# A Strassen block product for the last layer's gate and up projections

## The chip, the cores and the metric

The kernel runs on one core of one Trainium2 chip. The metric is the device time of one execution in microseconds (us). Before the change the median of three runs is 1853.85 us (1850.95 to 1854.17).

## The reference, cut to what matters

Two layers of a backbone over 512 latent tokens (and 256 context tokens, which the second layer's feed-forward does not need). Each layer is a mixer and a SwiGLU feed-forward; the change lies in the feed-forward of the second layer (called layer 1) and in what joins it to the mixer:

```
x = x + mod[2] * (o_lat @ w_out)                    # the mixer's output projection, 1024 -> 1024
h = modulate(rmsnorm(x, norm_ffn_w), mod[3], mod[4])
gate, up = split(h @ ffn_w_in)                      # 1024 -> 2 x 2816
x = x + mod[5] * ((silu(gate) * up) @ ffn_w_out)    # 2816 -> 1024
```

Everything is 32-bit. For TensorE the kernel splits each operand into a rounded high part and the remainder (tiles with h and l at the end of their names, type fp32r), and takes each product as three matmuls: high by high, high by low, low by high.

## The kernel before, in words

Tokens lie on the free axis, channels on the 128 partitions: 1024 channels are KD = 8 blocks `d`, the 2816 hidden channels are NH = 22 blocks. All matmuls are issued by the helper `mm` (L194), so they share that line; tensor_tensor operations of VectorE are recorded on L201, its scalar_tensor_tensor on L214, ScalarE's activations on L222, DMAs on L225 and the cast of a loaded weight to its high part on L251. Tiles are told apart by name: `wr` is a weight as it came from memory, `wh` and `wl` its split, `hx` the normalized input of a projection, `hf` a hidden block, `hhi` and `hlo` its split, `x` the residual stream, `mm` and `wk` PSUM tiles (four buffers each). A scheduler turns the program order into one instruction order per engine; each engine then works its own list strictly in order and waits on semaphores.

**The end of the mixer, `out_norm` (L625 to L692).** The output projection works on two token halves of NC = 256 columns: 8 blocks d, 8 k and 3 products of 256 columns each, for half 0 and then for half 1. Beside it run the weights' loads, the norm of half 0 (`stats`, `spread`), and `hx`, which for each block d makes the normalized, modulated input and its split. The norm of half 1 is left to a generator `rest`, which the feed-forward calls step by step.

**The feed-forward of layer 1, `ffn` (L1173 to L1244).** For each of 22 hidden blocks it loads the gate's and the up projection's weight (512 KB each), casts and splits them (ScalarE, VectorE), and makes 2 x 8 x 3 matmuls of 512 columns. Silu of the gate times up gives a hidden block, which is split again. Blocks are taken in groups of 8, 7 and 7 (`FFN_GROUPS`); `group_out` then multiplies a finished group with the output weights (8 blocks d, 3 matmuls of 512 for each hidden block of the group) and adds the result to the residual. It is put behind the second block of the next group. The first hidden block of all is done in two halves of 256 columns, since the norm of the second half comes later.

**Layer 0 does the same product in another way: `block_ffn` (L1313 to L1395).** There the tokens are two halves of HT = 384 columns, the 1024 input channels two halves of 4 blocks, and gate and up are the two halves of the output: a 2 x 2 block product. In place of 8 half-size products it makes 7 of them, by a Strassen scheme (product numbers 1, 2, 6, 7, 5, 4, 3 in the order of the program), each 4 k x 3 matmuls of 384 columns. Its price is sums: of the weights (`block_sums`: s1, s2, s3 and one in place, four additions of 128 x 512 per hidden block, and the splits of all of them), of the inputs (`block_operands`, once: 36 VectorE operations on half blocks after the normalized input stands) and of the results (copies `ha`, `hb` and additions out of PSUM). The feed-forward's input in layer 0 has to stand whole before the products that need sums of it can run.

Of the kernel before, what the change touches and what calls it, by code (L numbers as in the profile page):

```python
# [9 lines left out]
F32 = mybir.dt.float32  # L10
# [9 lines left out]
P = 128  # L20
D = 1024
KD = D // P
NL = 512
# [11 lines left out]
FFN_GROUPS = (8, 7, 7)  # L35
# [3 lines left out]
BLOCK_ROWS = 3  # L39
V_EARLY = (1,)  # L40
# [112 lines left out]
class Kern:  # L153
# [471 lines left out]
    def out_norm(self, pw, o, xt, sa, sb):  # L625
# [3 lines left out]
        act = ([], [])  # L629
        for d in range(KD):  # L630
            if d % 4 == 0:
                h = [K.t(K.bp, (P, 4, NT), "hx", F32R, bufs=4) for _ in range(2)]
            for a, x in zip(act, h):
                a.append(x[:, d % 4, :NL])
# [40 lines left out]
        for d in range(1, 4):  # L675
            out(1, d)
        r = spread(r)
# [4 lines left out]

        def rest():
            r = stats(1)
            yield
            r = spread(r)
            yield
            for d in range(KD):
                hx(1, r, d)
            yield  # L690

        return act, rest()  # L692
# [480 lines left out]
    def ffn(self, l, act, xt, regions, done=None, rest=None):  # L1173
        K = self
        lat = regions == 1
        n = NL if lat else NT
        pend = []
        hp = K.hp
        start = 0

        def group_out(g0, hs):
            for d in range(KD):
                nh = len(hs)
                w = K.wload(K.I["ffo"][l, d][:, g0:g0 + nh, :], (nh, P))
                pl = K.mmps()
                segs = [(pl, 0, NL, True)]
                if not lat:
                    pc = K.wkps()
                    segs = K.halves(pl, pc)
                K.proj_fm(w, ([x[0] for x in hs], [x[1] for x in hs]), segs)  # L1190
                g = K.modc[l][:, 40 + d, :]
                if lat:
                    K.stt(xt[:, d, :NL], pl, g[:, 0:1], xt[:, d, :NL])
                else:
                    for p, c, r in K.parts(pl, pc):
                        K.stt(xt[:, d, c], p, g[:, r:r + 1], xt[:, d, c])
                if done and g0 + nh == NH:
                    done(d)

        for gn in FFN_GROUPS:  # L1200
            hs = []
            for j in range(gn):
                if j == 2 and pend:
                    group_out(*pend.pop())
                ps, pcs = [], []
                late = []
                if rest:
                    next(rest)
                for gu in range(2):
                    w = K.wload(K.I["ffi"][l, start + j, gu], (KD, P))  # L1210
                    p = K.mmps()
                    segs = [(p, 0, NL, True)]
                    if rest:
                        segs = [(p[:, :NC], 0, NC, True)]
                        late.append((w, [(p[:, NC:], NC, NL, False)]))
                    if not lat:
                        pcs.append(K.wkps())
                        segs = K.halves(p, pcs[gu])
                    K.proj_fm(w, act, segs)
                    ps.append(p)  # L1220
                    if rest:
                        next(rest)
                if rest:
                    rest = None
                    for w, segs in late:
                        K.proj_fm(w, act, segs)
                f = K.t(hp, (P, n), "hf", bufs=2)
                if lat:
                    K.act(f, ps[0], AF.Silu)
                    K.mul(f, f, ps[1])  # L1230
                else:
                    for a in range(2):
                        c = slice(HT * a, HT * a + HT)
                        K.act(f[:, c], (ps, pcs)[a][0][:, :HT], AF.Silu)
                        K.mul(f[:, c], f[:, c], (ps, pcs)[a][1][:, :HT])
                hi = K.t(hp, (P, n), "hhi", F32R, bufs=10)
                lo = K.t(hp, (P, n), "hlo", F32R, bufs=10)
                K.A.copy(out=hi, in_=f)
                K.sub(lo, f, hi)
                hs.append((hi, lo))  # L1240
                K.bg(3, "mod")
            pend.append((start, hs))
            start += gn
        group_out(*pend.pop())  # L1244
# [702 lines left out]
```

## Time and profile before

| what | value |
|---|---|
| median of three runs | 1853.85 us (1850.95 to 1854.17) |
| the profiled execution | 1851.05 us, of which 1849.3 us lie between its first and last instruction |
| TensorE busy | 1765.9 us, 95% of the span |
| VectorE busy | 1192.7 us, 64% |
| ScalarE busy | 689.4 us, 37% |
| mean granted clock of TensorE | 0.973 of full speed |

The busy share is an average over the whole program. The change touches the last fifth of it: the output projection's last columns fall at 1480 us, and from there to the end VectorE works about a third of the time and TensorE is the only engine without gaps. A matmul's busy time is counted until its results are out, so two neighbours overlap in the records; what a matmul costs in a stream is the distance between starts.

### The profile page before, as it was taken

To read this page: it belongs to the slowest core of one execution; us is meant where nothing else is said; L and a number is where in the kernel's file an instruction comes from. 1 tells how busy PE (TensorE), PEld (TensorE's weight loads), DVE (VectorE), ACT (ScalarE), POOL (GpSimd) and SP (SyncE) were. 2 spreads that over 40 slices of the span, in tenths; PEclk is the share of its full clock that TensorE was granted. 3 is DMA by queue.
4 is the path that set the end of the run, shared out by engine and by line. 5 is a ranking of instruction groups with operands and counts; after the bars stand their busy time and mean duration, and the time that the engine had idled before them with its cause. 6 is when DMAs were issued, how large, how long until landed. Compare 5 with 4: busy or idle time off the path is not lost.

```text
span 1849.3 us, 28533 instructions
## 1 busy us (share of the span) xinstructions
PE 1765.9 (95%) x11047; PEld 1595.6 (86%) x11047; DVE 1192.7 (64%) x2422; ACT 689.4 (37%) x1417; POOL 87.1 (5%) x94
## 2 busy tenths in 40 slices
PE   4999999999899799999999998999999999999999
PEld 4988899988697799999999996788998988888887
DVE  5686696548847999988856467579555753333333
ACT  2453534235614642424242324322443432223231
POOL 0011001100002000000000000100003100000000
PEclk9999999779999899999999998999999999999999
DMA  8343466445374448496826265532532523333332
GB/s 334 113 153 125 125 212 187 99 153 185 112 226 184 167 129 284 163 313 207 284 89 199 72 213 193 182 109 74 176 110 93 182 80 93 101 94 96 99 95 96
DMA packets 123076, 286.71 MB, mean 155 GB/s; under 512 B 28729, under 2 KB 45545, under 8 KB 119228
## 3 DMA queue, kind: packets, MB, share of 16 engines
q1 hardware_dynamic: 122940, 284.88, 47.1%
q8 instruction: 87, 1.43, 0.3%
q14 instruction: 49, 0.40, 0.1%
HBM read 228.96 MB, written 55.87 MB: 154 GB/s over the span
## 4 chain that ended last, share of the span: by engine, by line
PE 76%; DVE 13%; DMA 5%; ACT 3%; issue 3%; POOL 0%; SPq 0%; POOLq 0%; DVEq 0%; ACTq 0%
PE mm L194 51%; PE wk L194 23%; DMA wm<-in_modt_dram 2%; PE wk L198 1%; DVE wj L214 1%; PE sa L194 1%; DVE wl L201 1%; DVE ac L214 1%; ACT wh L251 1%; PE sa L198 1%; DVE ul L201 1%; DVE x L201 1%; DVE ivt L201 0%; DMA rvt<-rvD 0%; DVE ivy L201 0%
## 5 line engine op out<-in xcount | busy, mean ns | idle before, releaser
L194 PE MATMUL mm<-hx,wh 128*128 128x512 f32 (+2 forms) x1976 | 526.5, 361 | 8.5 <-ACT hx L409 4.3
L194 PEld LDWEIGHTS mm<-hx,wh 128*128 128x128 f32 x1976 | 358.7, 190 | 54.2 <-ACT hx L409 4.5
L194 PE MATMUL mm<-hx,wl 128*128 128x512 f32 (+2 forms) x988 | 329.2, 360 | 0.5 <-DVE wl L201 0.5
L201 DVE TENSOR_TENSOR wl<-wr,wh 128x1024 fp32r<-128x1024 f32 (+1 forms) x159 | 193.3, 1215 | 186.4 <-ACT wh L251 178.6
L251 ACT CAST wh<-wr 128x1024 fp32r<-128x1024 f32 (+1 forms) x137 | 142.8, 1043 | 419.7 <-PE mm L194 411.6
L194 PE MATMUL mm<-wh,hx 128*128 128x256 f32 x1216 | 231.5, 289 | 2.6 <-DVE sv L964 1.1
L194 PEld LDWEIGHTS mm<-hx,wl 128*128 128x128 f32 x988 | 184.9, 190 | 23.6 <-issue 4.1
L194 PEld LDWEIGHTS mm<-wh,hx 128*128 128x128 f32 x1216 | 193.6, 194 | 5.5 <-issue 1.7
L194 PE MATMUL mm<-wl,hx 128*128 128x256 f32 x608 | 175.0, 289 | 0.0
L194 PEld LDWEIGHTS mm<-wl,hx 128*128 128x128 f32 x608 | 117.9, 194 | 1.0 <-issue 0.6
L1319 ACT CAST uh<-wr 128x512 fp32r<-128x512 f32 (+1 forms) x93 | 56.0, 605 | 155.6 <-PE wk L194 86.8
L214 DVE SCALAR_TENSOR_TENSOR wj<-wm,cb 128x1024 bf16<-128x1024 f32 x80 | 97.8, 1222 | 10.3 <-DMA wm<-in_modt_dram 9.8
L214 DVE SCALAR_TENSOR_TENSOR x<-mm,modc,x 128x256 f32<-128x256 f32 (+3 forms) x72 | 40.6, 585 | 86.2 <-PE mm L194 85.0
L194 PE MATMUL mm<-hx,uh 128*128 128x384 f32 x344 | 87.4, 334 | 0.6 <-ACT ha L1347 0.6
L201 DVE TENSOR_TENSOR ul<-wr,uh 128x512 fp32r<-128x512 f32 (+1 forms) x93 | 61.6, 665 | 18.5 <-ACT uh L1319 18.3
L194 PE MATMUL mm<-hhi,wh 128*128 128x512 f32 x176 | 68.5, 389 | 0.0
L194 PE MATMUL mm<-hlo,wh 128*128 128x512 f32 x176 | 68.5, 389 | 0.0
L194 PE MATMUL mm<-hhi,wl 128*128 128x512 f32 x176 | 68.5, 389 | 0.0
L1319 ACT CAST uh<-us 128x512 fp32r<-128x512 f32 x63 | 38.3, 623 | 76.8 <-PE wk L194 48.9
L194 PEld LDWEIGHTS mm<-hx,uh 128*128 128x128 f32 x344 | 62.0, 188 | 1.0 <-ACT ha L1347 1.0
L201 DVE TENSOR_TENSOR hf<-hf,mm 128x512 f32<-128x512 f32 x22 | 15.1, 688 | 71.6 <-PE mm L194 71.6
L194 PE MATMUL mm<-hlo,uh 128*128 128x384 f32 x176 | 58.9, 335 | 0.0
(447 smaller groups left out, 3426.8 us busy)
## 6 DMA issues: line engine op xcount, KB each, us to landing
wr<-in_ffi_dram SPq DMA_DIRECT2D x88, 512.0 KB
xr<-xr SPq DMA_DIRECT2D x80, 384.0 KB
wm<-in_modt_dram SPq DMA_DIRECT2D x56, 512.0 KB
wm<-in_modw_dram SPq DMA_DIRECT2D x20, 1024.0 KB
wr<-in_ffo_dram SPq DMA_DIRECT2D x32, 256.0 KB
wr<-in_rett_dram SPq DMA_DIRECT2D x16, 512.0 KB
wr<-in_ffo_dram SPq DMA_DIRECT2D x16, 448.0 KB
wr<-in_abf_dram SPq DMA_DIRECT2D x12, 512.0 KB
```

The source lines that it names most:

```text
L194: self.T.matmul(out=out, lhsT=l, rhs=r, start=start, stop=stop, skip_group_check=True)
L198: self.T.transpose(out, in_, self.ident[:n, :n])
L201: (eng or self.V).tensor_tensor(out=out, in0=a, in1=b, op=op)
L214: self.V.scalar_tensor_tensor(out=out, in0=a, scalar=s, in1=b, op0=op0, op1=op1, **kw)
L251: self.A.copy(out=hi, in_=raw)
L1319: A.copy(out=hi, in_=src)
```

## The change

`ffn` goes away. Layer 1's feed-forward is done by `block_ffn`, which now takes the half width as an argument (h = 384 in layer 0, NC = 256 in layer 1), the groups (6, 6, 5, 5 in layer 1), and the place of a finished group's output (behind the first block of the next group, `lead` = 1). `out_norm` builds the operands for the seven products instead of one input: half 0 gives the operands of products 1 and 2 while the second half of the output projection runs; the norm of half 1 is taken at once, and then `block_combos` makes the operands of 6, 7, 5, 4 and 3, in that order. The weights of a hidden block come from `block_pairs`, which casts and splits them in pieces of 1024, 512 and 1024 columns (tiles `f`, `e`, `f`); for hidden block 0 it is called inside the output projection.

```
-    def ffn(self, l, act, xt, regions, done=None, rest=None):
...
+    def out_norm(self, pw, hq, o, xt, sa, sb):
...
+        def split(n, k, x):
+            hi, lo = (o[:, k] for o in ops[n])
+            K.A.copy(out=hi, in_=x)
+            K.sub(lo, x, hi)
+
         def hx(t, r, d):
             c = slice(NC * t, NC * t + NC)
-            hd, ld = act[0][d][:, c], act[1][d][:, c]
-            x = K.t(K.sx, (P, NC), "hxt", bufs=4)
+            x = xp[d][:, c]
             K.stt(x, xt[:, d, c], sa[:, d, 0:1], r, ALU.mult, ALU.mult)
-            K.act(hd, x, AF.Identity, bias=sb[:, d, 0:1])
-            K.stt(ld, x, sb[:, d, 0:1], hd.bitcast(F32), ALU.add, ALU.subtract)
+            K.act(x, x, AF.Identity, bias=sb[:, d, 0:1])
+            if t == 0:
+                split(1 if d < 4 else 2, d % 4, x)
...
         for d in range(1, 4):
             out(1, d)
+        ready[0] = K.block_pairs(1, 0, hq)
         r = spread(r)
         for d in range(4, KD):
             out(1, d)
             for e in (2 * d - 8, 2 * d - 7):
                 hx(0, r, e)
...
+        r = spread(stats(1))
+        room((5, 4, 3))
+        for d in range(KD):
+            hx(1, r, d // 2 + 4 * (d % 2))
+        K.block_combos(xp, NC, split)
+        return ops, ready
...
+    def block_pairs(self, l, j, pool):
+        K = self
+        w, src, S, g = K.block_sums(l, j, pool, 2)
+
+        def split(x, n, tag):
+            hi, lo = (K.t(pool, (P, n, P), tag + c, F32R, bufs=2) for c in "hl")
+            K.A.copy(out=hi, in_=x)
+            K.sub(lo, x, hi)
+            return [(hi[:, i:i + 4], lo[:, i:i + 4]) for i in range(0, n, 4)]
+
+        w[6], w[7] = split(S[:, :8], 8, "f")
+        w[5], = split(src[5], 4, "e")
+        w[3], w[4] = split(src[0], 8, "f")
+        return w
...
-        for gn in BLOCK_GROUPS:
+        for gn in groups:
             hs = []
             for j in range(gn):
-                if j == 2 and pend:
+                if j == lead and pend:
                     group_out(*pend.pop())
...
-        act, rest = K.out_norm(K.pool(s, "wo", side="right"), od, xt, *K.scale_shift(1, "ffn", nr=1))
-        K.ffn(1, act, xt, 1, lambda d: K.dma(out[:, d], xt[:, d]), rest)
+        hq = K.pool(s, "hq1")
+        ops, ready = K.out_norm(K.pool(s, "wo", side="right"), hq, od, xt, *K.scale_shift(1, "ffn", nr=1))
+        K.block_ffn(1, NC, ready, ops, K.hp, hq, LAST_GROUPS, LAST_HID, 1, xt=xt, done=lambda d: K.dma(out[:, d], xt[:, d]))
```

The order of the instructions changes with it on VectorE and ScalarE; everything before `out_norm` keeps its order.

VectorE, in the second half of the output projection. Before, beside the additions to the residual (`x`) there stand the reciprocal root of half 0's norm (`nrst`, `nrsy`) and the split of the first gate weight (`wl`):

```order
L235 TENSOR_SCALAR nrst_14713<-nms_14711 128x2
L236 TENSOR_SCALAR nrsy_14714<-nrst_14713 128x2
L201 TENSOR_TENSOR nrst_14713<-nrsy_14714 128x2
L214 SCALAR_TENSOR_TENSOR nrst_14713<-nrst_14713,nms_14711 128x2
L214 SCALAR_TENSOR_TENSOR nrsy_14714<-nrst_14713,nrsy_14714 128x2
L214 SCALAR_TENSOR_TENSOR x_14514<-mm_14726,modc_10_88,x_14514 128x256
L201 TENSOR_TENSOR nrst_14713<-nrsy_14714 128x2
L214 SCALAR_TENSOR_TENSOR nrst_14713<-nrst_14713,nms_14711 128x2
L214 SCALAR_TENSOR_TENSOR nrsy_14714<-nrst_14713,nrsy_14714 128x2
L201 TENSOR_TENSOR wl_14902<-wr_14899,wh_14901 128x1024
```

Now, from the fifth addition of the first half on, the weight sums of hidden block 0 (`us` and, in place, the up weight `wr_14789`) and the splits of the sums (`el`, `fl`):

```order
L202 TENSOR_TENSOR us_14796<-wr_14789 128x512
L215 SCALAR_TENSOR_TENSOR x_14514<-mm_14635,modc_10_88,x_14514 128x256
L202 TENSOR_TENSOR us_14796<-us_14796,wr_14788 128x512
L202 TENSOR_TENSOR us_14796<-wr_14788,wr_14789 128x512
L215 SCALAR_TENSOR_TENSOR x_14514<-mm_14652,modc_10_88,x_14514 128x256
L202 TENSOR_TENSOR wr_14789<-wr_14788,us_14796 128x512
L202 TENSOR_TENSOR el_14806<-us_14796,eh_14805 128x512
L215 SCALAR_TENSOR_TENSOR x_14514<-mm_14669,modc_10_88,x_14514 128x256
L202 TENSOR_TENSOR fl_14802<-us_14796,fh_14801 128x1024
L215 SCALAR_TENSOR_TENSOR x_14514<-mm_14686,modc_10_88,x_14514 128x256
L202 TENSOR_TENSOR fl_14810<-wr_14789,fh_14809 128x1024
L215 SCALAR_TENSOR_TENSOR x_14514<-mm_14702,modc_10_88,x_14514 128x256
```

The sums and splits stand between the additions that empty the projection's PSUM tiles, and ahead of half 0's root.

VectorE, behind the norm of half 1. Before, the eight normalized inputs of half 1 (`hxt`) and their splits (`hx`):

```order
L214 SCALAR_TENSOR_TENSOR hxt_14964<-x_14514,saffn_2450_14532,wk_14930 128x256
L214 SCALAR_TENSOR_TENSOR hxt_14968<-x_14514,saffn_2450_14532,wk_14930 128x256
L214 SCALAR_TENSOR_TENSOR hxt_14972<-x_14514,saffn_2450_14532,wk_14930 128x256
L214 SCALAR_TENSOR_TENSOR hx_14553<-hxt_14964,modc_10_88,hx_14552 128x256
L214 SCALAR_TENSOR_TENSOR hx_14553<-hxt_14968,modc_10_88,hx_14552 128x256
```

Now, from the seventh of the eight inputs on (`hhi`, `hlo` are here the tiles that hold the input before it is split, `hxt` the sums for product 6, `hx` remainders of operands):

```order
L215 SCALAR_TENSOR_TENSOR hlo_14558<-x_14514,saffn_2450_14535,wk_14935 128x256
L215 SCALAR_TENSOR_TENSOR hlo_14562<-x_14514,saffn_2450_14535,wk_14935 128x256
L202 TENSOR_TENSOR hhi_14555<-hhi_14555 128x256
L202 TENSOR_TENSOR hlo_14556<-hlo_14556 128x256
L202 TENSOR_TENSOR hxt_2527_14956<-hhi_14559,hhi_14555 128x256
L202 TENSOR_TENSOR hxt_2528_14962<-hlo_14560,hlo_14556 128x256
L202 TENSOR_TENSOR hhi_14559<-hhi_14559,hxt_2527_14956 128x256
L202 TENSOR_TENSOR hx_14566<-hxt_2527_14956,hx_14565 128x256
L202 TENSOR_TENSOR hx_14566<-hxt_2528_14962,hx_14565 128x256
```

The inputs are followed by 36 operations of 256 columns without anything of another kind between them, the last of them the remainders of product 3's operand.

ScalarE, in the middle of the feed-forward. Before, a hidden block takes a silu, the cast of the hidden block and two casts of weights:

```order
L222 ACTIVATE hf_15044<-mm_14905 128x512
L251 CAST wh_15084<-wr_15082 128x1024
L1238 CAST hhi_15047<-hf_15044 128x512
L251 CAST wh_15122<-wr_15120 128x1024
L222 ACTIVATE hf_15113<-mm_15057 128x512
```

Now, for one block (PSUM copies `hf`, `ha`, `hb`, two silus, the cast of a hidden block, and casts of weights for this block and the next two):

```order
L1255 CAST fh_17234<-wr_17214 128x1024
L1255 CAST eh_17359<-us_17350 128x512
L1296 COPY hf_17241<-mm_17238 128x256
L1313 CAST hhi_17209<-hf_17112 128x512
L1301 COPY ha_17242<-mm_17238 128x256
L223 ACTIVATE hf_17241<-hf_17241 128x256
L1255 CAST fh_17355<-us_17350 128x1024
L1229 CAST wh_17475<-wr_17471 128x1024
L1304 COPY hb_17243<-mm_17238 128x256
L223 ACTIVATE hf_17241<-mm_17238 128x256
```

The copy `hb` out of PSUM, which product 3's matmuls into the same tile have to wait for, stands behind two casts of 1024 columns. On TensorE's list product 3 stands ahead of product 4, and between product 5 and it there are only some matmuls of the next block's product 1, nine here (4 to 10 in the blocks looked at).

## Rows read from the trace of the kernel before

**Rows 1.** The page, busy time, share of the span and instructions of each engine.

```profile
PE 1765.9 (95%) x11047; PEld 1595.6 (86%) x11047; DVE 1192.7 (64%) x2422; ACT 689.4 (37%) x1417; POOL 87.1 (5%) x94
```

**Rows 2.** The chain of waits that ended last: start, us, engine, tile, line, instructions.

```profile
1497.53 348.04 PE mm L194 x1534
```

**Rows 3.** Layer 1 by stretch: length, PE, PEld, DVE, ACT, POOL, clock, DMA, GB/s.

```profile
1480.00:1500.00 20.00, 17.45 (x121) 15.31 (x120) 16.17 (x41) 8.82 (x17) 0.73 (x1) 1.00 0.17 46
1500.00:1600.00 100.00, 100.00 (x443) 82.84 (x442) 33.67 (x36) 28.73 (x36) 0.00 (x0) 1.00 0.33 101
```

**Rows 4.** TensorE's timeline, streams of 256 and of 512 columns, and the last matmul.

```profile
1344.64 0.28 PE L194 MATMUL mm<-wl,hx 128*128 128x256 f32 x1
1344.76 0.40 PE L194 MATMUL mm<-wh,hx 128*128 128x256 f32 x2
1345.00 0.28 PE L194 MATMUL mm<-wl,hx 128*128 128x256 f32 x1
...
1528.28 0.39 PE L194 MATMUL mm<-hx,wl 128*128 128x512 f32 x1
1528.51 0.61 PE L194 MATMUL mm<-hx,wh 128*128 128x512 f32 x2
1528.96 0.39 PE L194 MATMUL mm<-hx,wl 128*128 128x512 f32 x1
...
1845.16 0.39 PE L194 MATMUL mm<-hhi,wl 128*128 128x512 f32 x1
```

**Rows 5.** VectorE's timeline at the end of the output projection.

```profile
1480.29 0.47 DVE L214 SCALAR_TENSOR_TENSOR x<-mm,modc,x 128x256 f32<-128x256 f32 x1
...
1482.95 0.16 DVE L218 TENSOR_SCALAR nms<-wk 128x2 f32<-128x2 f32 x1 [0.62 <-PE wk L194]
1483.02 1.22 DVE L201 TENSOR_TENSOR wl<-wr,wh 128x1024 fp32r<-128x1024 f32 x1
1484.16 0.88 DVE L214 SCALAR_TENSOR_TENSOR hx<-hxt,modc,hx 128x256 fp32r<-128x256 f32 x2
...
1487.94 1.26 DVE L214 SCALAR_TENSOR_TENSOR hxt<-x,saffn,wk 128x256 f32<-128x256 f32 x3 [0.87 <-PE wk L194]
1489.12 1.27 DVE L214 SCALAR_TENSOR_TENSOR hx<-hxt,modc,hx 128x256 fp32r<-128x256 f32 x3
```

**Rows 6.** DMA issues and the cast that waited, layer 0 and layer 1.

```profile
657.58 0.33 SPq L225 DMA_DIRECT2D wr<-in_ffi_dram  x1
...
661.47 1.06 ACT L1293 CAST wh<-wr 128x1024 fp32r<-128x1024 f32 x1 [1.78 <-DMA wr<-in_ffi_dram]
...
1458.94 0.42 SPq L225 DMA_DIRECT2D wr<-in_ffi_dram  x1
```

**Rows 7.** VectorE's timeline, the end of layer 0's operand sums.

```profile
619.33 0.56 DVE L201 TENSOR_TENSOR x<-hlo,x 128x384 fp32r<-128x384 f32 x1
619.80 1.90 DVE L201 TENSOR_TENSOR ul<-wr,uh 128x512 fp32r<-128x512 f32 x3
```

**Rows 8.** Busy time by stretch, layer 0: the front and the steady product.

```profile
605.00:610.00 5.00, 1.01 (x2) 0.50 (x2) 5.00 (x12) 5.00 (x13) 0.00 (x0) 0.54 0.57 229
610.00:615.00 5.00, 3.22 (x9) 2.75 (x10) 5.00 (x12) 5.00 (x13) 0.00 (x0) 0.50 0.64 205
615.00:620.00 5.00, 4.35 (x23) 3.83 (x21) 5.00 (x12) 4.42 (x4) 0.00 (x0) 0.94 0.35 137
645.00:694.00 49.00, 49.00 (x281) 48.29 (x280) 48.43 (x83) 21.86 (x39) 0.00 (x0) 1.00 0.42 132
```

**Rows 9.** ScalarE's timeline, layer 1's first block.

```profile
1495.17 1.05 ACT L251 CAST wh<-wr 128x1024 fp32r<-128x1024 f32 x1 [1.06 <-PE mm L194]
1496.12 0.59 ACT L222 ACTIVATE hf<-mm 128x512 f32<-128x512 f32 x1
```

**Rows 10.** TensorE's waits by releaser, layer 0's blocks, 630 to 1125 us, and one.

```profile
PE wk L194 <- DVE hb L201: 3.0, 4, 1.0
...
1027.28 0.30 PEld L194 LDWEIGHTS mm<-x,uh 128*128 128x128 f32 x2 [0.24 <-ACT hb L1350]
```

More of the change, by code (lines that the diff above doesn't have):

```diff
@@ L39 @@
 BLOCK_ROWS = 3
+LAST_GROUPS = (6, 6, 5, 5)
+LAST_HID = 8
 V_EARLY = (1,)
@@ L628, in out_norm, with room @@
         ws = [K.wget(), K.wget()] + [K.wload(K.I["cdo"][0][dp], (2, 4, P), pw) for dp in (2, 3)]
[L629 to L634, printed above, removed]
+        xp = [K.t(K.hp, (P, NL), ("hhi", "hlo")[d % 2], bufs=LAST_HID) for d in range(KD)]
+        ops = {7: [K.t(K.hp, (P, 4, NC), f"t7{x}", F32R, bufs=1) for x in "hl"]}
+        def room(ns):
+            hl = [K.t(K.bp, (P, 4, NT), "hx", F32R, bufs=4).rearrange("p a b -> p (a b)").rearrange("p (o k c) -> p o k c", o=3, k=4) for _ in range(2)]
+            for i, n in enumerate(ns):
+                ops[n] = [x[:, i] for x in hl]
+        room((1, 2, 6))
+        ready = {}
         acc = [K.t(K.sp, (P, NC), f"nacc{t}") for t in range(2)]
@@ L1171, in dn_out @@
             K.sub(ol[:, :, K.tok(i)], pv, oh[:, :, K.tok(i)])
-    def ffn(self, l, act, xt, regions, done=None, rest=None):
[L1174 to L1202, printed above, removed]
-                if j == 2 and pend:
[L1204 to L1244, printed above, removed]
@@ L1271, in block_operands, with block_combos @@
         ops[4], ops[3] = (xs[:, 0], xs[:, 1]), (xs[:, 2], xs[:, 3])
+        K.block_combos(xp, h, split)
+        return ops
+    def block_combos(self, xp, h, split):
+        K = self
         for k in range(4):
@@ L1284, in block_operands, with block_sums @@
                 split(n, k, xp[d + k][:, c:c + h])
-        return ops
-    def block_sums(self, l, j, pool):
+    def block_sums(self, l, j, pool, bufs=1):
         K = self
@@ L1311, in block_first, with unit, block_units, block_ffn @@
         return w, {5: g[:, :4], 4: src[4], 3: src[3]}
-    def block_ffn(self, l, first, ops, hp, hq, xr):
-        K, A = self, self.A
-        h = HT
-        def unit(src, n=4):
-            hi, lo = (K.t(hq, (P, 4, P), "u" + x, F32R, bufs=6)[:, :n] for x in "hl")
-            A.copy(out=hi, in_=src)
-            K.sub(lo, src, hi)
-            return hi, lo
-        def weights(j):
-            w, src = K.block_sums(l, j, hq)[:2] if j else first
-            for m in (6, 7, 5, 4, 3):
-                if m in src:
-                    w[m] = unit(src[m])
-            return w
+    def block_pairs(self, l, j, pool):
+        K = self
+        w, src, S, g = K.block_sums(l, j, pool, 2)
[8 more added lines that the diff above has]
+        return w
+    def unit(self, pool, src, n=4):
+        hi, lo = (self.t(pool, (P, 4, P), "u" + x, F32R, bufs=6)[:, :n] for x in "hl")
+        self.A.copy(out=hi, in_=src)
+        self.sub(lo, src, hi)
+        return hi, lo
+    def block_units(self, pool, w, src):
+        for m in (6, 7, 5, 4, 3):
+            if m in src:
+                w[m] = self.unit(pool, src[m])
+        return w
+    def block_ffn(self, l, h, ready, ops, hp, hq, groups, hid, lead, xr=None, xt=None, done=None):
+        K, A = self, self.A
+        def weights(j):
+            if j in ready:
+                return ready.pop(j)
+            return K.block_units(hq, *K.block_sums(l, j, hq)[:2]) if xr else K.block_pairs(l, j, hq)
         def product(ps, w, m, first=False):
@@ L1357, in hidden @@
             K.mul(f[:, h:], f[:, h:], b)
-            hi, lo = (K.t(hp, (P, NT), t, F32R, bufs=BLOCK_HID) for t in ("hhi", "hlo"))
+            hi, lo = (K.t(hp, (P, 2 * h), t, F32R, bufs=hid) for t in ("hhi", "hlo"))
             A.copy(out=hi, in_=f)
@@ L1368, in group_out @@
             last = g0 + nh == NH
-            if last:
+            if last and xr:
                 xt = K.t(K.bp, (P, KD, NT), "x", bufs=1)
@@ L1373, in group_out @@
                 K.dma(raw, K.I["ffo"][l, d][:, g0:g0 + nh, :])
-                w = unit(raw, nh)
+                act = [t[0] for t in hs], [t[1] for t in hs]
+                if not xr:
+                    hi, lo = (K.t(K.wp, (P, KD, P), n, F32R, bufs=2)[:, :nh] for n in ("wh", "wl"))
+                    A.copy(out=hi, in_=raw)
+                    K.sub(lo, raw, hi)
+                    pl = K.mmps()
+                    K.proj_fm((hi, lo), act, [(pl, 0, NL, True)])
+                    K.stt(xt[:, d, :NL], pl, K.modc[l][:, 40 + d, 0:1], xt[:, d, :NL])
+                    if last:
+                        done(d)
+                    continue
+                w = K.unit(hq, raw, nh)
                 x = xt[:, d] if last else K.t(hq, (P, NT), "xr", bufs=BLOCK_ROWS)
@@ L1377, in group_out @@
                 pl, pc = K.mmps(), K.wkps()
-                K.proj_fm(w, ([t[0] for t in hs], [t[1] for t in hs]), K.halves(pl, pc))
+                K.proj_fm(w, act, K.halves(pl, pc))
                 for p, c, r in K.parts(pl, pc):
```

19 lines of the change are left out of this document (3 added, 16 removed).

## The prediction

> **What bounds the kernel now.** I read the page's busy times first. TensorE is busy for 1765.9 of 1849.3 us and issues one weight load per matmul, 11047 of each [rows 1], so it is the engine to look at; but that is an average, and the change lies behind 1480 us. The windows there show TensorE without a gap at full clock from 1500 to 1600 us, with VectorE at 33.67 and ScalarE at 28.73 of 100 us [rows 3]. The chain of waits ends in one piece of 348.04 us of matmuls, 1534 of them, from 1497.53 us on, without a single wait in it [rows 2]. So in this stage the number and the size of matmuls set the time, and VectorE and ScalarE have room. The timeline gives the price: at 512 columns three matmuls start in 0.68 us (1528.28 to 1528.96), 0.2267 us each; at 256 columns three in 0.36 us (1344.64 to 1345.00), 0.12 us each [rows 4].
>
> **What is removed and added on TensorE.** Before, a hidden block takes 48 matmuls of 512 columns, 10.88 us; the first takes 96 of 256, 11.52 us: 21 x 10.88 + 11.52 = 240.0 us. After, each takes 7 products x 4 k x 3 = 84 matmuls of 256 columns, 10.08 us, 22 of them 221.8 us. That is 18.2 us less. The output product is the same in both (22 x 8 x 3 = 528 matmuls of 512, 119.7 us); other groups only cut it elsewhere. 18.2 us is the most that the change can give.
>
> The 256-column price comes from another stage, and here the Trainium skill speaks against the change. By "TensorE: Matmul & The Clock Gate", section "Back-to-back issue gap", a stream of weight loads and matmuls is spaced 81 ns at 128 columns and 131 ns at 512; on a line between, an estimate, 256 columns take 98 ns, a block 8.2 us in place of 6.3, and the change costs 42 us. The isolated gap of the same section, N/2.4 + 2.5 ns, gives 109 and 216 ns, and a gain of 26 us. The trace, with 226.7 and 120 ns, agrees with neither, so the sum goes by its rows.
>
> **What there is before.** The last addition of the output projection starts at 1480.29 us [rows 5]; the last matmul starts at 1845.16 us, so the stream ends at 1845.39 us [rows 4]. Between lie 365.1 us for 240.0 + 119.7 = 359.7 us of matmuls: 5.4 us idle, all before 1497.53 us, while half 1's norm and input are made. Behind the last matmul come 3.9 us to the end of the span, and 1.75 us lie around it.
>
> **The front after the change.** This is where I expect the gain to go.
>
> *The norm of half 1.* VectorE is busy for 16.17 of the 20 us from 1480 us [rows 3] and has about 8 us of room in the projection before. Into this come block 0's sums and, behind them, part of block 1's. A 512-column operation adds 0.60 us (three in 1.90, less 0.09 of overlap), a 1024-column one about 1.13 (the split of a weight, 1483.02 to 1484.16) [rows 5, 7]: four sums, the lo of 512 and two lo of 1024 are 5.3 us for each block, and some 4.1 us net of the split that stood there. Block 0's sums hide in the room: four PSUM tiles stand between TensorE and the additions. Of block 1's some 1.8 us lie in the way of the root. The loads matter too: VectorE waits in order, and a load takes 3.9 us from issue (657.58 to 661.47 us, the cast that waits for it [rows 6]). Block 0's up weight has the slot at 1458.94 us, there at 1463, just about in time. Block 2's up weight needs a buffer that comes free about 1486.3 us, is there at 1490.2, and the first sum that reads it stands ahead of the eight inputs. So the eight inputs begin at about 1490.8 us; before they began at 1487.94 us [rows 5].
>
> *The operands.* Then VectorE runs eight inputs at 0.40 us (three in 1.19, 1487.94 to 1489.12 us [rows 5]) = 3.2 us, and 36 operations of 256 columns. No row has these alone: 384 columns step by 0.47 us (619.33 to 619.80 us), 512 by 0.60 [rows 7], so 256 take about 0.34, 12.2 us in all (at least 24/36 of the 384 price, 11.3; at most the whole, 16.9). With 1 us of waits for ScalarE's casts the last operand stands at 1490.8 + 3.2 + 12.2 + 1 = 1507.2 us, and block 0's product 3, the last that needs it, ends at about 1508.5 us.
>
> *What TensorE does meanwhile.* It has products 1 and 2, and 6, 7, 5 and 4 as their operands come, of blocks 0 and 1: 8 products and two matmuls by 1508.5 us, 11.8 us of work in 28.2 us. That is 16.4 us idle in place of 5.4, a loss of 11.0 us. Layer 0's front is the picture of it: there VectorE and ScalarE are 100% busy for 10 us, TensorE for 1.01 and 3.22 us, and the granted clock falls to 0.50, back to 0.94 in the next 5 us [rows 8]. I expect the same from about 1488 to 1504 us here. While TensorE waits for operands half clock costs nothing; it costs when the matmuls become dense. Bounds for the front: 6 us idle (norm of half 1 undelayed, inputs at 1487.9 us, clock full, most products hidden under the chain) to 22 us (loads late twice, half clock some 6 us into the dense stretch). I take 16.4, nearest to layer 0's rows.
>
> **The steady blocks.** In the 10.08 us of a block VectorE has four sums and one lo of 512 (5 x 0.60), three lo of 1024 (3.4), three PSUM additions (1.2), two products (0.7) and the hidden block's lo (0.60): 8.9 us, 88%, against a third before. Layer 0's window has 48.43 of 49.00 us of VectorE and TensorE without a gap [rows 8], so a full VectorE alone does no harm. ScalarE has 5.5 us (0.95 for each cast of 1024 [rows 9]). Loads stay at 1 MB a block, 104 GB/s against 101 [rows 3]. The new wait is product 3 on the copy `hb` of tile `mm`. The copy stands behind the casts `fh`, whose buffer comes free when product 7 ends, and `wh`: 0.95 + 0.95 and some 0.25 us for the copy, 2.15 us from product 7's end. TensorE has product 5 meanwhile, 1.44 us, and 4 to 10 matmuls of the next block, 0.48 to 1.2 us: 1.92 to 2.64 us. Behind the waiting matmul stand products 4 and all of the next block. In layer 0 the same copy cost TensorE at most a few tenths (0.24 us at 1027.28 us), and its blocks show 3.0 us of waits in four cases over 20 blocks [rows 10]. Bounds: nothing, to 0.7 us in each of 21 blocks, 15 us (cover 1.44 us alone). I take 2.5 us in all, nearest to layer 0's 3.0.
>
> **The sum.** 1480.3 + (221.8 + 119.7) + 16.4 + 2.5 = 1840.7 us for the last matmul; with 3.9 us of tail and 1.75 us around the span 1846.35 us, 4.7 us under the profiled execution's 1851.05 us. That one is 2.8 us under the median of the runs, so the forecast is 1853.85 - 4.7 = 1849.2 us, 0.25% faster. From the bounds its own range is 1842 to 1854 us.
>
> **Rivals.**
> - *A wash.* The front costs 4.7 us more than I say, or the blocks lose (4.7 + 2.5)/21 = 0.34 us each. For it: layer 0's clock stayed low for ten microseconds, and the chain there was the same; in a block three casts of 1024 stand in ScalarE's list between PSUM copies. Against: the clock's return in rows 8 within 5 us. About 1854 us, between 1850 and 1857.5.
> - *Slower: VectorE becomes the bound.* One mechanism: VectorE works in order, and each wait of it (for a cast of ScalarE, for a product in PSUM) is time that 88% hardly leaves. It decides when a block's waits pass 10.08 - 8.9 = 1.2 us. With 1.8 us a block takes 10.7 us, 20.3 blocks x 0.62 = 12.6 us; in place of the 2.5 this gives 1849.2 + 10.1 = 1859.3 us. For it: in rows 5 VectorE stands 0.62 and 0.87 us at two such places. Against: layer 0's VectorE is 99% busy, so there its waits nearly vanish [rows 8].
> - *Small matmuls pay for their own weight load.* If 256 columns couldn't hide it, the price would rise to a load's mean busy time, 1595.6/11047 = 0.144 us; break-even is at 10.88/84 = 0.1295 us. Against: the row at 0.12 us is a stream with one load to each matmul [rows 1, 4]. At 0.144 us it is 1848 x 0.024 = 45 us more than the forecast, 1894 us. The skill's sustained spacing belongs here.
> - *The change does not do what it says*: the products run but block 0's sums displace the projection's additions. That is the upper end of the front's bound, and in the wash.
>
> **Chances.** Forecast 0.57, wash 0.26, VectorE the bound 0.15, weight loads 0.02. 0.2% is 3.7 us, about what a measurement of this kernel can tell. The forecast lies 1 us beyond it and its range is lopsided to the good, since most of its 12 us lies there: of its 0.57 I give 0.50 to faster and 0.07 to the same. So faster 0.50, same 0.07 + 0.26 = 0.33, slower 0.17. The range 1842 to 1858 us holds the forecast's own, the wash, and the milder half of the VectorE case.
>
> **What would show it.** Right: 1848 matmuls of 256 columns at 0.12 us between 1480 us and the end; the first dense stretch at about 1508 us with low granted clock in some of the 15 us before, VectorE full there; then blocks of 10.1 to 10.3 us, VectorE near 9 us in each, and few waits of `mm` on the copy `hb`. Wrong: gaps in every block ahead of product 3 (wash), VectorE without idle time and blocks over 10.6 us (the slower case), a 256-column step above 0.13 us, or a front that is full before 1500 us (then the gain is 10 us and more).

## The result: slower, by about half a percent

The changed kernel took 1867.09 us (median of 5, 1860.99 to 1868.03) against 1853.85 us: ratio 1.0057, 95% interval 1.0038 to 1.0077. Run once more with ten executions it took 1860.96 us, ratio 1.0046 (1.0030 to 1.0062). Forecast were 1849.2 us and 0.25% faster. The direction was wrong, and both medians lie outside the range of 1842 to 1858 us.

Its profiled execution took 1868.03 us, 16.98 more than that of before. More than half of this lies ahead of the change. One landmark is in both kernels: VectorE's first addition of the output projection. Up to it VectorE, ScalarE and GpSimd work the same instructions in the same order in both traces; only the lengths of their waits differ. Before reached it at 1459.02 us, the changed kernel at 1468.32, 9.3 us later. From it to the end of the span it took 390.3 us before and 398.0 after: in these two traces 7.7 us lie behind the landmark, where the programs differ.

The page of the changed kernel, busy time by engine [rows 1]:

```profile
PE 1768.9 (95%) x11791; PEld 1632.0 (87%) x11791; DVE 1321.4 (71%) x2686; ACT 756.2 (41%) x1585; POOL 88.2 (5%) x94
```

744 more matmuls and 264 more VectorE operations, and TensorE's busy share stays at 95%: the average shows nothing. The timeline does. VectorE before, the first, fourth and eighth addition of the output projection, from the fourth on one every 1.4 us, each waiting for its product only (start, us; the bracket is the idle time before, and who ended it):

```profile
1459.02 1.26 DVE L214 SCALAR_TENSOR_TENSOR x<-mm,modc,x 128x256 f32<-128x256 f32 x3
1460.87 0.48 DVE L214 SCALAR_TENSOR_TENSOR x<-mm,modc,x 128x256 f32<-128x256 f32 x1 [0.59 <-PE mm L194]
...
1466.50 0.48 DVE L214 SCALAR_TENSOR_TENSOR x<-mm,modc,x 128x256 f32<-128x256 f32 x1 [0.93 <-PE mm L194]
```

And in the changed kernel, with the issue of the up weight's load (SPq):

```profile
1468.32 0.87 DVE L215 SCALAR_TENSOR_TENSOR x<-mm,modc,x 128x256 f32<-128x256 f32 x2
...
1468.97 0.42 SPq L226 DMA_DIRECT2D wr<-in_ffi_dram  x1
...
1469.38 0.48 DVE L215 SCALAR_TENSOR_TENSOR x<-mm,modc,x 128x256 f32<-128x256 f32 x1 [0.19 <-PE mm L195]
1470.82 0.48 DVE L215 SCALAR_TENSOR_TENSOR x<-mm,modc,x 128x256 f32<-128x256 f32 x1 [0.95 <-PE mm L195]
1474.45 0.69 DVE L202 TENSOR_TENSOR us<-wr 128x512 f32<-128x512 f32 x1 [3.15 <-DMA wr<-in_ffi_dram]
1475.06 0.48 DVE L215 SCALAR_TENSOR_TENSOR x<-mm,modc,x 128x256 f32<-128x256 f32 x1
1475.46 0.68 DVE L202 TENSOR_TENSOR us<-us,wr 128x512 f32<-128x512 f32 x1
1476.05 0.69 DVE L202 TENSOR_TENSOR us<-wr,wr 128x512 f32<-128x512 f32 x1
1476.66 0.48 DVE L215 SCALAR_TENSOR_TENSOR x<-mm,modc,x 128x256 f32<-128x256 f32 x1
...
1480.09 0.47 DVE L215 SCALAR_TENSOR_TENSOR x<-mm,modc,x 128x256 f32<-128x256 f32 x1
...
1498.00 0.48 DVE L215 SCALAR_TENSOR_TENSOR x<-mm,modc,x 128x256 f32<-128x256 f32 x1
```

The first sum of block 0 waits 3.15 us for its up weight, and the additions stand behind it; then each has a sum or split in front of it. The eighth (1480.09) is 11.8 us behind the first; before it was 7.5. And it is not the wait alone. From first to last addition, before and after (length; busy PE, PEld, DVE, ACT, POOL; clock; DMA, GB/s):

```profile
1459.02:1480.29 21.27, 20.67 (x174) 20.26 (x172) 14.64 (x40) 9.85 (x22) 9.00 (x12) 1.00 0.34 106
1468.32:1498.00 29.68, 26.25 (x193) 25.62 (x191) 22.13 (x50) 14.01 (x31) 10.35 (x12) 0.88 0.29 98
```

VectorE's own work there rose from 14.64 to 22.13 us, more than the 21.27 us that the whole projection took before. Each addition is squared on ScalarE and accumulated on GpSimd (`nacc`), and half 0's norm matmul on TensorE reads that:

```profile
1480.80 1.01 PE L195 MATMUL wk<-cst,nacc 128*128 128x1 f32 x4 [2.96 <-POOL nacc L202]
...
1483.31 0.63 PE L195 MATMUL mm<-hx,wh 128*128 128x256 f32 x2
1483.74 0.41 PE L195 MATMUL mm<-hx,wl 128*128 128x256 f32 x1
1483.95 0.63 PE L195 MATMUL mm<-hx,wh 128*128 128x256 f32 x2
...
1488.68 0.40 PE L195 MATMUL mm<-hx,wh 128*128 128x256 f32 x2
1488.92 0.28 PE L195 MATMUL mm<-hx,wl 128*128 128x256 f32 x1
1489.04 0.40 PE L195 MATMUL mm<-hx,wh 128*128 128x256 f32 x2
...
1531.08 0.28 PE L195 MATMUL mm<-hx,el 128*128 128x256 f32 x1
...
1531.43 0.28 PE L195 MATMUL mm<-hx,el 128*128 128x256 f32 x1
```

TensorE waits 2.96 us, and for 6 us afterwards three matmuls take 0.64 us (1483.31 to 1483.95) in place of 0.36 (1488.68 to 1489.04): the granted clock has fallen to the lower of its two levels, 1.2 of 2.4 GHz. The windows show it, 0.55 on the mean of 1480 to 1485 us, and again while the operands are made (columns as above) [rows 3, 8]:

```profile
1475.00:1480.00 5.00, 2.84 (x25) 2.64 (x23) 5.00 (x9) 3.56 (x6) 2.34 (x3) 1.00 0.02 10
1480.00:1485.00 5.00, 4.20 (x19) 4.20 (x20) 2.55 (x6) 0.83 (x2) 0.75 (x1) 0.55 0.33 108
1485.00:1490.00 5.00, 5.00 (x36) 5.00 (x35) 4.19 (x13) 2.24 (x3) 0.73 (x1) 0.76 0.10 16
...
1505.00:1510.00 5.00, 3.75 (x16) 3.49 (x16) 3.77 (x12) 2.03 (x6) 0.00 (x0) 0.50 0.17 69
1510.00:1515.00 5.00, 1.90 (x6) 1.43 (x6) 4.84 (x15) 5.00 (x16) 0.00 (x0) 0.50 0.00 2
1515.00:1520.00 5.00, 4.56 (x19) 4.26 (x20) 5.00 (x16) 3.61 (x10) 0.00 (x0) 0.50 0.02 5
1520.00:1525.00 5.00, 5.00 (x37) 4.89 (x37) 4.71 (x12) 2.26 (x4) 0.00 (x0) 0.85 0.00 0
...
1536.00:1546.00 10.00, 10.00 (x84) 9.81 (x83) 9.65 (x16) 6.36 (x11) 0.00 (x0) 1.00 0.38 125
```

Behind the projection the front looks as forecast. VectorE there [rows 5, 7]:

```profile
1505.57 0.16 DVE L215 SCALAR_TENSOR_TENSOR nrsy<-nrst,nrsy 128x2 f32<-128x2 f32 x1
1506.85 0.69 DVE L202 TENSOR_TENSOR us<-wr 128x512 f32<-128x512 f32 x1 [1.12 <-DMA wr<-in_ffi_dram]
1507.46 0.87 DVE L215 SCALAR_TENSOR_TENSOR hhi<-x,saffn,wk 128x256 f32<-128x256 f32 x2
...
1510.60 0.42 DVE L202 TENSOR_TENSOR hhi<-hhi 128x256 f32<-128x256 f32 x1
...
1522.59 0.43 DVE L202 TENSOR_TENSOR hx<-hlo,hx 128x256 fp32r<-128x256 f32 x1
```

In the steady blocks the new wait is there, small and often. TensorE's waits for the copy `hb` (us in total, times, longest) [rows 10]:

```profile
PEld mm L195 <- ACT hb L1304: 5.4, 20, 0.5
PE mm L195 <- ACT hb L1304: 0.9, 4, 0.3
```

One of them in the timeline of ScalarE and TensorE:

```profile
1562.11 1.05 ACT L1229 CAST wh<-wr 128x1024 fp32r<-128x1024 f32 x1 [0.32 <-DMA wr<-in_ffi_dram]
1563.06 0.36 ACT L1304 COPY hb<-mm 128x256 f32<-128x256 f32 x1
...
1563.48 0.30 PEld L195 LDWEIGHTS mm<-hx,fh 128*128 128x128 f32 x2 [0.27 <-ACT hb L1304]
```

Here the copy stands behind the cast of 1024 columns, which itself waited 0.32 us for its load; the weight load of TensorE's next product waits for the copy.

### The profile page after: what moved, and what is told of

Its sections match the earlier page's. It is cut to its first block, busy times and chain, and to the rows that moved or that the text cites. A ratio compares the mean times of both kernels' runs of the same rounds, so it can differ in the third digit from the quotient of the medians.

```text
span 1866.3 us, 30503 instructions
## 1 busy us (share of the span) xinstructions
PE 1768.9 (95%) x11791; PEld 1632.0 (87%) x11791; DVE 1321.4 (71%) x2686; ACT 756.2 (41%) x1585; POOL 88.2 (5%) x94
## 5 line engine op out<-in xcount | busy, mean ns | idle before, releaser
L195 PE MATMUL mm<-hx,wh 128*128 128x384 f32 (+2 forms) x1416 | 346.1, 345 | 7.5 <-ACT hx L410 3.5
L195 PEld LDWEIGHTS mm<-hx,wh 128*128 128x128 f32 x1416 | 254.5, 194 | 26.7 <-issue 3.9
L202 DVE TENSOR_TENSOR wl<-wr,wh 128x1024 fp32r<-128x1024 f32 (+2 forms) x145 | 167.6, 1156 | 110.3 <-ACT wh L252 100.9
L195 PE MATMUL mm<-hx,wl 128*128 128x384 f32 (+2 forms) x708 | 216.1, 343 | 0.0
L195 PEld LDWEIGHTS mm<-hx,wl 128*128 128x128 f32 x708 | 134.3, 193 | 9.6 <-issue 4.1
L252 ACT CAST wh<-wr 128x1024 fp32r<-128x1024 f32 x69 | 72.7, 1053 | 168.2 <-PE mm L195 162.7
L215 DVE SCALAR_TENSOR_TENSOR x<-mm,modc,x 128x512 f32<-128x512 f32 (+3 forms) x80 | 46.6, 600 | 62.8 <-PE mm L195 62.8
L195 PE MATMUL wk<-hx,wh 128*128 128x384 f32 (+1 forms) x352 | 79.9, 315 | 1.3 <-DVE hx L202 1.2
L195 PE MATMUL mm<-hx,fh 128*128 128x256 f32 x352 | 70.0, 294 | 5.6 <-ACT hx L670 3.8
L195 PEld LDWEIGHTS mm<-hx,fh 128*128 128x128 f32 x352 | 55.5, 193 | 11.4 <-ACT hb L1304 5.4
```

The costliest lines, as they stand in the source:

```text
L195: self.T.matmul(out=out, lhsT=l, rhs=r, start=start, stop=stop, skip_group_check=True)
L202: (eng or self.V).tensor_tensor(out=out, in0=a, in1=b, op=op)
L215: self.V.scalar_tensor_tensor(out=out, in0=a, scalar=s, in1=b, op0=op0, op1=op1, **kw)
L252: self.A.copy(out=hi, in_=raw)
```

## The experiments

All of them are read by the same two distances: from the projection's first addition to its last, and to the end of the span (us, from one trace each).

| kernel | first addition at | to the last | to the end |
|---|---|---|---|
| before | 1459.0 | 21.3 | 390.3 |
| before, again | 1454.3 | 22.0 | 390.9 |
| before with the change's groups | 1466.3 | 22.0 | 391.0 |
| changed | 1468.3 | 29.7 | 398.0 |
| changed, again | 1457.6 | 26.2 | 393.6 |
| call moved in the code | 1468.6 | 26.0 | 393.9 |
| weights in buffers of their own | 1461.9 | 30.8 | 399.8 |
| third buffer for f | 1457.5 | 28.7 | 394.9 |
| no load of block 0's up weight | 1465.8 | 26.5 | 394.7 |
| no sums for block 0 | 1459.3 | 27.4 | 392.7 |
| sums held behind the projection | 1461.4 | 21.5 | 394.6 |
| block 0 plain | 1462.3 | 27.7 | 391.3 |
| block 0 plain, sums held | 1460.9 | 24.2 | 388.9 |
| blocks 0 and 1 plain | 1466.4 | 22.9 | 383.1 |

The changed kernel's own two traces differ by 3.5 us in the projection and by 4.4 us to the end. So the variants that stand clear of it are few: in the projection those at 24.2 us or less, to the end those at 388.9 us or less. The ends between 391.3 and 399.8 us tell nothing by themselves.

**How much is luck: both kernels again.** 

> The changed kernel itself, once more. Theory N (part of the 13 us by which it was slower at first is luck of the execution in the code before the projection, which is the same in both kernels): median 1860 to 1864 us, 7 to 9 us above the kernel before, as the end counted from the projection's first addition says (398.0 against 390.3); the first addition anywhere from 1457 to 1469 us; that addition to the last 26 to 31 us again. Rival P (the 13 us are the kernel's own): 1866 to 1868 us, first addition at 1466 us or later.

> The kernel before itself, once more with a trace. Theory N (the time to reach the projection moves from execution to execution, what comes behind it is the kernel's own): from the first addition of the projection to the end 389 to 391 us again (390.3 in the first trace, 391.0 in the kernel with other groups), projection 21 to 22 us, while the first addition may lie anywhere from 1455 to 1469 us. Rival P: the first addition within 1 us of 1459.0, and then the end as well.

The changed kernel's median was 1860.96 us; its traced execution took 1853.09 us, 15 less than the first one traced, with the first addition at 1457.6. Before had its first addition at 1454.3 us and 390.9 us from there, median 1853.89 (ratio 1.0001, 0.9985 to 1.0017). Theory N holds as far as this: with the same instructions in the same order the projection is reached between 1454 and 1469 us, at 1466.3 in a kernel of the old kind too. Whether the changed program also reaches it later on average is open: 1459.9 us is the mean of three traces of the old kind, 1462.7 of eleven of the new one, which is within this spread. The rest is steady in the kernels of the old kind (390.3, 390.9, 391.0) and not in the changed one (398.0, 393.6).

**The call elsewhere in the code.**

```
-        ready[0] = K.block_pairs(1, 0, hq)
         r = spread(r)
...
         r = spread(stats(1))
+        ready[0] = K.block_pairs(1, 0, hq)
```

> The changed kernel with the call that makes block 0's weight sums moved in the code from inside the output projection to behind it, behind the root of half 1's norm. The order of the instructions hardly moves (VectorE's sums stay between the same additions of the projection, since the scheduler goes by readiness), so this is nearly the changed kernel itself. Theory A (VectorE's wait for block 0's up weight, with the projection's additions behind it, costs the projection some 8 us): the wait of about 3 us is there again, the projection takes about 33 us from its first matmul to its last addition, against 25 before, and the time is about 1867 us. Rival N (the extra 9 us with which the changed kernel reached the projection, in code whose order did not change, is luck of the execution): the projection is reached anywhere between 1455 and 1465 us, and the time moves with that. Rival P (those 9 us belong to the change's program, by its length or its places in memory): it is reached at 1462 us or later.

Ratio 1.0047 (1.0029 to 1.0065), 1863.77 us. VectorE waited 2.18 us for the up weight, the projection took 26.0 us from its first addition, 3.7 less than the changed kernel's first trace. (The expectations of this run and the next count from the first matmul, some 3.4 us earlier.) Where the call stands shows no effect.

**An early load that was not early.** Block 0's weights got their own tiles (`w0g`, `w0u`), loaded at the start of `out_norm`:

```
+        gu = K.block_load(1, 0, hq, "w0", 1)
...
+        ready[0] = K.block_pairs(1, 0, hq, gu)
```

> The changed kernel with block 0's two weights in buffers of their own, so that their load does not wait until a weight of the output projection has been split; the scheduler then also puts the first sum three additions later in VectorE's order. Theory A: without VectorE's wait of 3.15 us the accumulation of the squares on GpSimd and the norm's matmuls on TensorE come in time, the granted clock stays at full speed in the projection, which takes 25 to 27 us in place of 33; time about 1859 us. Rival B (the sums themselves, 5 us of VectorE work between the additions, hold the projection up, not the load): the projection stays at 31 us or more, time 1865 to 1868 us.

Ratio 1.0058 (1.0037 to 1.0079). The loads were now issued behind those of block 1, and VectorE waited as long as before, so this run does not separate the theories; it only shows the same loss with another tile:

```profile
1472.15 0.69 DVE L202 TENSOR_TENSOR us<-w0u 128x512 f32<-128x512 f32 x1 [3.04 <-DMA w0u<-in_ffi_dram]
```

**Load or sums.** Block 0's up weight replaced by its gate weight (`u = g`), or no sums at all:

```
+        w1, w2 = (gh[:, :4], gl[:, :4]), (gh[:, 4:], gl[:, 4:])
+        ready[0] = {1: w1, 2: w2, 6: w1, 7: w2, 5: w1, 4: w2, 3: w1}
```

> The changed kernel with block 0's sums made from the gate weight alone: its up weight is not loaded (block 0's result is another one), the sums and splits stay, and stand where they can. Theory A (VectorE's wait for the second load is what holds up the projection): from the projection's first addition to its last 21 to 24 us, against 21.3 before and 26 to 31 in the changed kernel and its variants. Rival B (the sums and splits between the additions hold it up): 26 us or more. The end counted from the projection's first addition: A 391 to 393 us, B 395 to 398 (before 390.3, changed 398.0).

> The changed kernel without block 0's weight sums: all its products use the split gate weight (block 0's result is another one), so neither the up weight's load nor the sums and their splits are there. Theories A and B both expect the projection back at 21 to 23 us from first to last addition; together with the run without the second load this divides the loss into load and sums. If it stays above 25 us, neither is the cause, but the operands of half 0 and the sums of block 1. End from the first addition: 390 to 392 us.

26.5 and 27.4 us, as long as in the changed kernel's second trace: theory A is wrong, since the wait for the up weight is not needed for the loss, and B is wrong as far as it means block 0's sums alone. Ratios 1.0044 (1.0027 to 1.0061) and 1.0029 (1.0011 to 1.0046). The trace without the up weight, from first to last addition:

```profile
1465.82:1492.30 26.48, 23.52 (x194) 22.84 (x192) 24.94 (x53) 14.24 (x31) 11.38 (x12) 1.00 0.31 110
```

VectorE waited for a load once, for 0.69 us, and the clock stayed at full speed; but it was busy for 24.94 of the 26.48 us. The sums' own work is enough for some 5 us. The trace without block 0's sums shows what took their place, VectorE and then TensorE:

```profile
1466.96 0.69 DVE L202 TENSOR_TENSOR us<-wr 128x512 f32<-128x512 f32 x1 [1.88 <-DMA wr<-in_ffi_dram]
...
1470.49 0.61 PE L195 MATMUL wk<-cst,nacc 128*128 128x1 f32 x4 [1.68 <-POOL nacc L202]
```

These are block 1's sums. VectorE's list has the next sums at hand there, whichever block's they are; they take its time, and one whose load is under way stops everything behind it as well. In the three traces with sums in the projection whose clock stayed at 1.00 (call moved, no up weight, no sums) it took 26.0 to 27.4 us; in the five whose mean clock there fell to 0.88 to 0.93 it took 26.2 to 30.8 us. That the fallen clock makes this difference is likely, and no run tests it by itself.

**Sums kept out of the projection.** The two tiles of the sums are taken by a dummy, released by an operation that reads the last addition's result:

```
+        held = [K.t(hq, (P, 12, P), "us", bufs=2) for _ in range(2)]
...
+        for i, t in enumerate(held):
+            K.add(junk[:, i:i + 1], t[:, 0, :1], xt[:, KD - 1, NC:NC + 1])
```

> The changed kernel, whole, but the tiles of the first two blocks' sums are taken by a dummy until behind the projection's last addition (two 4-byte operations more), so that no sum of weights stands between the projection's additions; nothing else is changed. Theory D (VectorE, which works in order, reaches a sum whose weight is still on the way, and with it wait the projection's additions, GpSimd's accumulation of the squares and TensorE's norm matmuls, whichever block's sums they are): projection back to 21 to 23.5 us from first to last addition, no TensorE wait for nacc above 1 us in its middle; behind it the front is up to 5 us longer than the changed kernel's, since the sums now stand there; end from the first addition 389 to 395 us (before 390.3, changed 398.0, its variants 392.7 to 399.8). Rival E (something else of the change holds the projection up: the casts on ScalarE, the loads' traffic, the inputs of half 0): projection still 26 us or more.

Theory D holds for the projection: 21.5 us, and no wait for `nacc` over 0.84 us, as before (0.8). The run takes the sums' work and their waits for loads out together, so it does not divide the two. But the end is at 394.6 us, ratio 1.0039 (1.0017 to 1.0061). First and last addition, and TensorE behind them:

```profile
1461.43 1.26 DVE L215 SCALAR_TENSOR_TENSOR x<-mm,modc,x 128x256 f32<-128x256 f32 x3
...
1482.92 0.47 DVE L215 SCALAR_TENSOR_TENSOR x<-mm,modc,x 128x256 f32<-128x256 f32 x1
...
1493.48 0.58 PE L195 MATMUL mm<-hx,wl 128*128 128x256 f32 x1 [7.37 <-DVE wl L202]
```

TensorE now waits 7.37 us behind the projection for a split that stands behind the sums. From the last addition to the end it is 373.1 us against 368.3: of the 8.2 us won in the projection 4.8 are given back. Against the changed kernel's second trace (26.2 and 367.4) 4.7 us are won and 5.7 given back, and the medians (1861.18 and 1860.96) show no gain. The sums cost in both places tried.

**Groups, and the copy.** `FFN_GROUPS = (6, 6, 5, 5)` with the output behind the first block, in the kernel before; and `bufs=3` for the splits `f` in the changed one.

> The kernel before with the change's groups (6, 6, 5, 5 in place of 8, 7, 7) and the finished group's output behind the first block of the next group: the part of the change that has nothing to do with the products. Theory A (grouping costs nothing, all of the loss lies in the norm, the operands and the sums): same as before, within 2 us of 1853.85. Rival C (the shorter groups cost by themselves, by 8 more output steps with their loads and additions): 3 us slower or more. For the arrival at the projection: by rival P (length or places of the program) it may differ from 1455 us here too, by N any of 1453 to 1465.

> The changed kernel with three buffers in place of two for the pair splits f, so that ScalarE's cast of the next pair need not wait for the end of product 7, and the copy hb no longer stands right behind that. Theory A (in the steady blocks TensorE's waits for the copy hb, 5.4 us in 20 waits, come from the casts in front of the copy): the waits for hb fall to under 2 us, time 3 to 5 us less than the changed kernel, about 1863 us. Rival B (the copy waits for anything else on ScalarE): waits for hb stay at 4 to 6 us and the time at 1867.

The groups cost 0.7 us by the trace, about what two traces of before differ by (0.6); ratio 1.0012 (0.9990 to 1.0033): nothing that can be told. With three buffers TensorE's waits for `hb` fell from 6.3 to 3.8 us, and 2.2 us of waits for the copy `ha` came; from the first block's cast to the last addition it took 331.2 us in place of 333.2. Ratio 1.0019 (1.0000 to 1.0038). So 2 of the expected 3 to 5 us, by one trace each: the casts in front are one cause of the waits, and 3.8 us have another that was not looked for.

**A way to win.** The first blocks as plain gate and up products in two token halves, with weights that need no sums; half 1's inputs split first, the operands' sums behind; three buffers for `f`:

```
+        for d in range(KD):
+            hx(1, r, d)
+            split(0 if d < 4 else 3, d % 4, xp[d][:, NC:])
+        second = [[ops[0 if k < 4 else 3][i][:, k % 4] for k in range(KD)] for i in range(2)]
+        for w, p in late:
+            K.proj_fm(w, second, [(p[:, NC:], 0, NC, False)])
+        K.block_combos(xp, NC, split, (3,))
```

> A way to win: block 0 as plain gate and up products in two token halves (96 matmuls of 256 columns, as before the change), whose first half needs only the split input of half 0, and whose weights need no sums; the inputs of half 1 are split first and the sums of the operands come behind; blocks 1 to 21 by the seven products; three buffers for f. Theory A (what the change loses is VectorE's sums in the projection, 6 us, and TensorE's idle 16 us until the operands stand): projection 22 to 24 us, TensorE's idle time in front about 8 us less, 1.4 us more of matmuls; end from the first addition 386 to 388 us, 3 us better than before. Rival: the idle time only moves behind the first block, because the operands come later by 3 us: 391 us, no better than before.

> The kernel with block 0 as plain products and the sums of blocks 1 and 2 kept behind the projection in the same way. Theory D: projection 22 to 24 us in place of that kernel's 27.6, end from the first addition 386 to 389 us, 2 to 4 us better than before. Rival E: 27 us and 391 us again.

> The same with blocks 0 and 1 as plain products in two halves (2.9 us more of matmuls than the changed kernel): 11.5 us of work for TensorE before half 1's norm, and 11.5 us behind it beside the operands' sums. Theory A: TensorE is idle under 6 us in front, the clock stays at full speed; end from the first addition 382 to 385 us, 5 to 8 us better than before, 0.3 to 0.4% faster. Rival: buffers of the weights (two for the splits, three for f) come free too late behind the plain blocks and block 2 waits for its weights: 388 to 391 us, within 0.2% of before.

One plain block: 1.0023 (1.0007 to 1.0039); block 1's sums moved into the projection, as the runs on load and sums explain (27.7 us). That run's 386 to 388 us were missed. With those sums held: 24.2 and 388.9 us, by the trace 1.4 us less than before, ratio 1.0009 (0.9987 to 1.0030), so nothing by the timed executions. Two plain blocks: 1849.69 us against 1853.40, ratio 0.9965 (0.9948 to 0.9981), faster than both kernels. No sums stand in its projection (22.9 us), and TensorE has work while the operands are made, with 0.83 as the lowest mean clock of these windows:

```profile
1485.00:1495.00 10.00, 9.35 (x80) 9.14 (x79) 8.76 (x23) 7.04 (x20) 2.63 (x4) 1.00 0.04 7
1495.00:1505.00 10.00, 7.98 (x55) 7.81 (x54) 8.91 (x29) 5.53 (x16) 0.00 (x0) 0.83 0.13 49
1505.00:1515.00 10.00, 10.00 (x86) 10.00 (x85) 8.46 (x26) 7.96 (x21) 0.00 (x0) 1.00 0.00 0
1515.00:1525.00 10.00, 9.33 (x76) 8.92 (x75) 10.00 (x19) 4.81 (x9) 0.00 (x0) 1.00 0.21 68
```

## Why the prediction was wrong, step by step

- *The stream of matmuls, 18.2 us less.* Right: 256 columns cost 0.12 us here too (1488.68 to 1489.04; 0.35 us for three at 1531.08 to 1531.43). The weight-load rival is out. By the Trainium skill, "TensorE: Matmul & The Clock Gate", section "Back-to-back issue gap", the step would be 109 ns as an isolated gap, or 98 ns as an estimate on a line between its sustained figures; this trace bears out neither. (The loss of 42 us that the prediction worked out from these sustained figures of the Trainium skill is 39 us, an estimate too, when the first block before is counted with its 96 matmuls of 256 columns.)
- *Block 0's sums hide in VectorE's room in the projection.* This step failed. It was priced at nothing and cost 8.4 us in the first trace (29.7 against 21.3), 4.9 in the second (26.2). The "about 8 us of room" came from no row: before, VectorE was idle for 6.6 us between first and last addition (21.27 less 14.64), and the change put 7.5 us more work there (22.13 us in all). I had also written that the up weight's load would be there "just about in time" from its 3.9 us in layer 0. In this place it took 5.5 us from issue to sum (1468.97 to 1474.45), and at 3.9 us too VectorE, which was through with the fourth addition at 1471.30, would have waited some 1.6 us. And I counted four PSUM tiles as cover, but not the other chain from the additions: squares, GpSimd, the norm's matmul in TensorE's own order, and the clock.
- *Half 1's norm, inputs, operands.* Right to 2 us: 25.0 us from the last addition to the last operand (1498.0 to 1523.0), 26.9 forecast; block 2's late load stood there as foreseen (1.12 us); half clock from 1505 to 1520 us, and TensorE lost 16.6 us of these 25 against 16.4 forecast (it ran 66 matmuls of 256 columns and some small ones in them, by my estimate 8.4 us of work at full clock).
- *Steady waits, 2.5 us.* The mechanism was right, the size not: the waits on copies and splits behind 1526 us sum to some 7.5 us, 6.3 of them for `hb`, about 0.3 us a block. In the case shown the weight's cast in front of the copy waits for its load too, which I had not counted; what holds the copy in the others is open.
- *VectorE the bound (rival).* Not seen in the blocks, where it was priced: VectorE was busy for 9.65 of 10 us from 1536 us on, and TensorE for all 10. VectorE's work bounds the output projection instead (24.94 of 26.48 us busy in the run without the up weight), the place for which the forecast had named cover.
- *A wash (rival).* It asked for 4.7 us more in the front, or 0.34 us lost in each block. The blocks alone met it, with 7.5 us of waits, 0.36 us each over 21 blocks, and the 8.4 us in the projection came on top: so the end lies beyond this rival too. Sums that displace the projection's additions were named, under the last rival, but counted into the front's bound and the wash, with no price or chance of their own.
- *The sum.* -4.7 forecast, +8.4 projection, +5.0 steady, and -1.0 that is left over for the front (16 of the feed-forward's matmuls, 1.9 us, ran before the last addition): +7.7 us, as traced. The 9.3 us before the landmark come on top in that execution. In the second one the own part was 3.3 us.

How the medians of the timed executions (7 to 13 us above before) divide between own part and luck stays open: only traced executions have the landmark. (Each half of the projection has 4 k, 96 matmuls; the description ahead says 8.)

## What to carry to other kernels

An operation that is put into an engine's idle time is free only if the idle time, read from a row of that very stretch, holds it, and if its input is there. An engine that works in order passes both its time and its wait on to everything behind it, so price it by who reads the results of the operations behind it. Taking one such operation out may let the next of its kind move up; keep the whole kind out, and give the next engine other work meanwhile, as the two plain blocks do. And compare executions from a landmark where the two programs part, before explaining a difference of some microseconds.

## What was not expected of the chip

The same instructions in the same order reached the same point between 1454.3 and 1468.6 us in 14 traces. Up to there VectorE's waits for loads sum in the two first traces to 29.7 us (24 waits) before and 33.5 us (23 waits) after, with 1.70 against 3.58 us at one weight of the modulation near 840 us; from 800 to 900 us the loads ran at 267 and 251 GB/s. The granted clock goes with it: 88.7 us at its lower level up to the landmark in the traces that reach it at 1454.3 and 1457.6 us, 116.1 us in those that reach it at 1468.3 and 1468.6. Which of the two comes first, and why the loads' speed differs from execution to execution, was not tested.
